# Moving an inverse to VectorE's transposes, a norm to a block's delay, and a last norm to fused steps

## The chip, the core and the metric

One NeuronCore of one Trainium2 chip runs the whole program. The time is device microseconds from start to end of an execution, the median of some runs. The engines work side by side, each through its own queue in order: TensorE (PE, with PEld for its weight loads), VectorE (DVE), ScalarE (ACT), GpSimd (POOL), and SyncE (SP), which issues most DMAs. [...]

## What is computed

One layer of a backbone on 640 tokens, 128 of a prompt and 512 of a sample, 1024 features, fp32:

```python
h = x * (1 + sc1) + sh1
proj = h @ p['w_in']
q, k, v, rw, gates = jnp.split(proj, ...)
o_att = diff_attention(q, k, v, lam)          # 4 heads, then rms_norm
# bidirectional RWKV7, 8 heads of 64, for each direction and token:
sa = jnp.einsum('bhvk,bhk->bhv', S, a_t)
S = S * w_t[:, :, None, :] + sa[..., None] * b_t[:, :, None, :] + v_t[..., None] * k_t[:, :, None, :]
y_t = jnp.einsum('bhvk,bhk->bhv', S, r_t)
...
mix = (ga * (o_att @ p['w_o_attn']) + gb * o_rw) @ p['w_out']
x = layer_norm(ALPHA * x + g1 * mix, p['ln1_g'], p['ln1_b'])
h = x * (1 + sc2) + sh2
u, val = jnp.split(h @ p['w_up'], 2, axis=-1)
u = prev * cw[0] + u * cw[1] + nxt * cw[2] + p['conv_b']
f = (jax.nn.gelu(u) * val) @ p['w_down']
x = layer_norm(ALPHA * x + g2 * f, p['ln2_g'], p['ln2_b'])
```

Outputs are x of both token groups, the prompt's keys and values, and the final states S of both directions.

## The kernel before

Tokens stand in five blocks of 128 (block 0 is the prompt). Matrix operands are split into a high and a low part, so that a product is three: high by high, high by low, low by high.

**The mixing stage** (about 60 to 710 us) interleaves two kinds of work on PE by hand. One is the input projection: a generator `flow` that yields after each product (L215, 128x320), and `pull(n)` takes n of them. These products are the fillers here. The other is the scan, in four pairs of heads, i = 0 to 3. The scan is chunked: 64 tokens a chunk, 10 chunks a direction, so 40 chunk matrices a pair (two heads, two directions). Each needs the inverse of a triangular 64x64 matrix. In the loop over pairs:

- `rw_b` (through `side()`) prepares decays and keys; `rw_c` multiplies them into the 40 chunk matrices (L642) and masks them on VectorE (L648) into the tile MS, 128 partitions x 40 chunks x 128.
- `rw_i` inverts the two 32x32 diagonal blocks of each chunk matrix. 64 products with the identity (L706) turn the blocks so that chunks lie on partitions (X, 104 partitions: chunks of one block on 0 to 39, of the other on 64 to 103); 4 copies evict them (L710). 60 VectorE operations (L716, L718) eliminate. 8 PE transposes (L729) and 16 copies (L733, half on ACT) bring the blocks back into MS. Between the 30 elimination steps stand a `side()` and a `pull(4)`.
- `rw_m` joins the blocks (transpose L741, products L747 and L755), forms the chunk operators and walks the states (L839, L841), ten steps with `pull(14)` each. It ends with the final states' transposes (L864), a copy fo and two DMAs to new_s.
- `rw_e` forms the outputs y (L888), `rw_d` the transposed operands, `rw_f` the norm of the scan's output (L899 to L923), which it writes to yr_dram.

`side()` advances the first of the listed side generators until it is done. After the loop `rw_e(3)`, `pull(12)`, and `rw_f(3)` with `pull(8)` a step run, then what is left of the fillers. Then the stage's pools are closed, and attention loads queries and keys (L1097) and starts with L1086 and L1116.

**The first norm.** `w_out`'s second half of columns is multiplied for the five blocks (L1249), each into a PSUM bank of its own. For each block follow the residual (L1277, L1278), the statistics, the norm itself (L1326, on VectorE), 8 transposes (L1332) and the operands oph and opl of the up-products (L1335 to L1343, L224). A scheduler fixes the order on each engine when the program is built, from the order of the code and its own estimates. The first up-products are L1413.

**The last norm.** The down weights come in groups of 5, 5, 5 and 7 blocks of 128. For the last group's second half of columns 2 of 7 blocks go over all five token blocks first, the other 5 (TJS) keep their weights in tiles (wdh, wdl) and run token block by token block (L1447 to L1449), and `finish` then does each block's norm: L1461, L1462, statistics, nm, and per half L1476 (ACT, once L1474 on VectorE), L1477 (VectorE), L1478 (VectorE for the five halves listed in BD, else GpSimd), and a DMA out.

Of the kernel before, what the change touches and what calls it, by code (L numbers as in the profile page):

```python
# [47 lines left out]
TJS = 5  # L48
# [18 lines left out]
def tile_layer(ctx, tc, x_prompt, x_sample, cache_k, cache_v, state_rwkv, c, c_ctx, w_ada, b_ada, w_in,  # L67
# [625 lines left out]
    def rw_i(i):  # L693
        MS = R[i]["MS"]

        X = rp.tile([104, 32, 32], F32, name="X", tag="st")
        tmp = rp.tile([104, 256], F32, name="tmpx", tag="tmpx")
        nc.gpsimd.memset(X[32:64], 0.0)
        prev = None
# [24 lines left out]

        for y in (1, 0):
            ps = bank(psR, "m", 2)
            for u in (3, 2, 1, 0):
                c0 = 128 * (4 * y + u)
                prev = chain(prev, pq(nc.tensor.transpose(out=ps[:, 104 * u:104 * u + 104], in_=Xf[:, c0:c0 + 128], identity=ident[0:104, 0:104])))  # L729
            for q in range(4):  # L730
                for b in range(2):
                    t0 = 32 * b + 16 * y + q
                    (nc.scalar.copy if b else nc.vector.tensor_copy)(  # L733
                        out=MS[32 * b:32 * b + 32, :, t0:t0 + 13:4],
                        in_=ps[32 * q:32 * q + 32, 0:416].rearrange("p (u r) -> p r u", u=4)[:, 64 * b:64 * b + 40, :])
        pull(16)

    def rw_m(i):
# [104 lines left out]
        for v in range(10):  # L843
# [16 lines left out]
            pull(14)  # L860
        ps = bank(psR, "m", 2)
        fo = rp.tile([64, 2, P], F32, name="fo", tag="tmpx")
        for d in range(2):
            pq(nc.tensor.transpose(out=ps[0:64, d * P:(d + 1) * P], in_=FS[:, d, :], identity=ident))  # L864
        nc.scalar.copy(out=fo, in_=ps[0:64, 0:256].rearrange("p (d k) -> p d k", d=2))
        for d in range(2):
            nc.sync.dma_start(out=new_s[d, 2 * i:2 * i + 2].rearrange("e v k -> v e k"), in_=fo[:, d, :].rearrange("p (e k) -> p e k", e=2))

        R[i].update(UV=UV, ST=ST)

    def rw_e(i):
# [18 lines left out]
        R[i].update(y=y, gup=gup)  # L890

# [704 lines left out]
```

## Time and profile before

| | |
|---|---|
| median of 3 runs | 1432.46 us (1431.22 to 1436.12) |
| the profiled execution | 1437.26 us, its span 1435.2 us, mean granted clock of PE 0.932 |
| PE busy | 1287.7 us, 90% of the span |
| VectorE busy | 911.8 us, 64% |
| ScalarE, GpSimd busy | 563.7 and 564.9 us, 39% each |
| chain that ended last | PE 38%, VectorE 16%, issue 5%, GpSimd 4%, ScalarE 3%, DMA 2% |

Times in rows are microseconds from the start of the span. The span is about 2 us shorter than the execution's own time. A PE row's duration covers the whole pipeline, so that rows follow each other faster than they last: the step from one start to the next is what a product costs. Idle time in brackets stands ahead of an instruction, with the instruction that ended it. [...]

### The profile page before, as it was taken

Reading aid. Unit: us, or ns where it says so; the run is one execution under the profiler, and the core shown is the slowest. Engines: PE = TensorE matmul, PEld = TensorE weight load, DVE = VectorE, ACT = ScalarE, POOL = GpSimd, SP = SyncE. Lnnn points to the kernel's source line nnn. Section 1 sums busy time; section 2 is a strip of 40 time slices with the busy share of each in tenths; the row PEclk is TensorE's granted clock in tenths of the full one; section 3 lists DMA queues with packets and bytes.
Section 4 is the critical chain, followed back from the end, with each engine's and each line's share of the span. In section 5 each row is a group of like instructions: output and inputs, shape, how many; then the busy total and the mean of one; then the engine's idle time right before and its main releaser. Section 6 shows DMA issues by size and latency. Waiting matters only on the chain.

```text
span 1435.2 us, 27691 instructions
## 1 busy us (share of the span) xinstructions
PE 1287.7 (90%) x11105; PEld 1140.6 (79%) x11105; DVE 911.8 (64%) x1683; ACT 563.7 (39%) x1158; POOL 564.9 (39%) x424
## 2 busy tenths in 40 slices
PE   6998898988888999999979889968999999999994
PEld 5887887877777888889867777758988989989983
DVE  2365847584847563831266523597897987778777
ACT  3442533344324441533355412354543433434432
POOL 3252217331643232212220235546654735536623
PEclk9997998898988998999989999978999999999997
DMA  9411212220222111212656787513232232322222
GB/s 306 125 49 34 63 30 69 78 76 28 64 72 70 51 33 51 77 50 75 195 160 204 265 265 265 171 60 102 74 104 73 74 96 66 90 66 79 69 67 88
DMA packets 157459, 144.64 MB, mean 101 GB/s; under 512 B 10490, under 2 KB 128020, under 8 KB 157332
## 3 DMA queue, kind: packets, MB, share of 16 engines
q1 hardware_dynamic: 147490, 127.85, 29.0%
q10 hardware_dynamic: 9842, 15.03, 3.1%
q8 instruction: 87, 1.43, 0.4%
q14 instruction: 40, 0.33, 0.1%
HBM read 121.06 MB, written 19.69 MB: 98 GB/s over the span
## 4 chain that ended last, share of the span: by engine, by line
PE 38%; DVE 16%; issue 5%; POOL 4%; ACT 3%; DMA 2%; SPq 0%; ACTq 0%; DVEq 0%; POOLq 0%
PE ps_d L1413 8%; PE ps_d L215 6%; PE ps_x L215 4%; PE ps_e L1413 3%; PE acc L1449 2%; PE acc L1447 2%; PE acc L1448 2%; DVE sums L1386 2%; DVE zacc L1462 1%; PE acc L1249 1%; PE T L1140 1%; POOL wl L224 1%; DMA ws<-in_w_out_dram 1%; DVE X L718 1%; DVE tmpx L716 1%
## 5 line engine op out<-in xcount | busy, mean ns | idle before, releaser
L187 POOL TENSOR_TENSOR wl<-ws,wh 128x512 fp32r<-128x512 f32 x100 | 138.5, 1386 | 400.5 <-ACT wh L186 349.4
L224 POOL TENSOR_TENSOR wl<-sums,wh 128x512 fp32r<-128x512 f32 x88 | 137.4, 1568 | 38.3 <-ACT wh L223 36.5
L1413 PE MATMUL ps_d<-oph,wh 128*128 128x320 f32 x440 | 138.5, 315 | 10.6 <-DVE u L1425 5.0
L224 POOL TENSOR_TENSOR wl<-wu,wh 128x512 fp32r<-128x512 f32 x63 | 88.9, 1412 | 142.9 <-ACT wh L223 129.6
L1413 PE MATMUL ps_d<-oph,wl 128*128 128x320 f32 x440 | 137.5, 313 | 0.6 <-POOL wl L224 0.6
L1413 PE MATMUL ps_d<-opl,wh 128*128 128x320 f32 x440 | 137.3, 312 | 0.7 <-DVE opl L224 0.7
L186 ACT CAST wh<-ws 128x512 fp32r<-128x512 f32 x100 | 61.4, 618 | 171.3 <-PE ps_d L215 66.9
L215 PE MATMUL ps_x<-hl,wh 128*128 128x320 f32 (+1 forms) x304 | 104.5, 344 | 0.0
L215 PE MATMUL ps_x<-hh,wh 128*128 128x320 f32 (+1 forms) x304 | 104.5, 344 | 0.0
L215 PE MATMUL ps_x<-hh,wl 128*128 128x320 f32 (+1 forms) x304 | 104.2, 343 | 0.0
L215 PE MATMUL ps_d<-hl,wh 128*128 128x320 f32 (+1 forms) x304 | 103.7, 341 | 0.0
L215 PE MATMUL ps_d<-hh,wl 128*128 128x320 f32 (+1 forms) x304 | 103.6, 341 | 0.0
L215 PE MATMUL ps_d<-hh,wh 128*128 128x320 f32 (+1 forms) x304 | 103.4, 340 | 0.0
L1413 PEld LDWEIGHTS ps_d<-oph,wh 128*128 128x128 f32 x440 | 83.7, 190 | 15.1 <-ACT wh L223 7.7
L1413 PEld LDWEIGHTS ps_d<-opl,wh 128*128 128x128 f32 x440 | 83.7, 190 | 2.0 <-POOL hf L1343 1.1
L1413 PEld LDWEIGHTS ps_d<-oph,wl 128*128 128x128 f32 x440 | 83.7, 190 | 1.4 <-POOL wl L224 1.2
L223 ACT CAST wh<-sums 128x512 fp32r<-128x512 f32 x88 | 54.6, 620 | 65.2 <-PE ps_e L1413 25.4
L1447 PE MATMUL acc<-wh,gh 128*128 128x512 f32 x195 | 77.5, 398 | 2.6 <-ACT gh L223 2.6
L1448 PE MATMUL acc<-wl,gh 128*128 128x512 f32 x195 | 77.3, 397 | 0.0
L1449 PE MATMUL acc<-wh,gl 128*128 128x512 f32 x195 | 76.1, 397 | 0.5 <-DVE gl L224 0.5
L223 ACT CAST wh<-wu 128x512 fp32r<-128x512 f32 x63 | 39.1, 621 | 73.2 <-PE acc L1449 30.1
L215 PEld LDWEIGHTS ps_x<-hh,wh 128*128 128x128 f32 x304 | 63.4, 209 | 2.6 <-issue 1.1
(439 smaller groups left out, 3641.2 us busy)
## 6 DMA issues: line engine op xcount, KB each, us to landing
wu<-in_w_up_dram SPq DMA_DIRECT2D x42, 512.0 KB
ws<-in_w_in_dram SPq DMA_DIRECT2D x76, 256.0 KB
wa<-in_w_ada_dram SPq DMA_DIRECT2D x24, 512.0 KB
ws<-in_w_down_dram SPq DMA_DIRECT2D x44, 256.0 KB
wa<-in_w_ada_dram SPq DMA_DIRECT2D x8, 1024.0 KB
ks<-qk_dram SPq DMA_DIRECT2D x32, 192.0 KB
g_dram<-tg ACTq DMA_DIRECT2D x16, 320.0 KB
tg<-g_dram SPq DMA_DIRECT2D x16, 320.0 KB
```

Of the source, the lines that this page charges most:

```text
L186: nc.scalar.copy(out=wh, in_=ws)
L187: (lo_eng or nc.gpsimd).tensor_tensor(out=wl, in0=ws, in1=wh.bitcast(F32), op=ALU.subtract)
L215: pq(nc.tensor.matmul(pd, w[:, k, :], x[:, g, sl], start=g == 0 and z == 0, stop=g == kb - 1 and z == 2))
L223: nc.scalar.copy(out=hi, in_=src)
L224: (lo_eng or nc.vector).tensor_tensor(out=lo, in0=src, in1=hi.bitcast(F32), op=ALU.subtract)
L716: nc.vector.tensor_tensor(out=tv, in0=X[:, j:j + 1, 0:j].broadcast_to([104, n, j]), in1=X[:, j + 1:32, j:j + 1].broadcast_to([104, n, j]), ...
L718: nc.vector.tensor_tensor(out=X[:, j + 1:32, 0:j], in0=X[:, j + 1:32, 0:j], in1=tv, op=ALU.add)
L1386: (nc.vector if q in USM else nc.gpsimd).tensor_tensor(out=o, in0=x0, in1=x1, op=op)
L1413: nc.tensor.matmul(ps, w[:, k, :], x[:, b, k, :], start=k == 0 and z == 0, stop=k == 3 and z == 2)
L1447: nc.tensor.matmul(acc, a_h, wh, start=first, stop=False)
L1448: nc.tensor.matmul(acc, a_h, wl, start=False, stop=False)
L1449: nc.tensor.matmul(acc, a_l, wh, start=False, stop=last)
```

## The change

1. `rw_i`: the 64 products, the 4 copies, the 8 PE transposes and the 16 copies are gone. Four stream transposes on VectorE turn the blocks into X, four turn them back. Each takes 32 partitions x 32 chunks x 32; a chunk lies 512 bytes from the next in MS, while X is contiguous. X has 128 partitions now, four groups: chunks 0 to 31 and 8 to 39 of each diagonal block, so that 24 chunks are inverted twice. The elimination's free sizes stay. A `pull(8)` stands behind each of the four first transposes (before, four times 6), and `pull(26)` at the end (16).
2. `side()` takes the side generators in turn.
3. `rw_m` pulls 16 instead of 14 fillers a step. Its last part, transposes of the final states, copy and DMAs, stands at the end of `rw_e`.
4. `pull(40)` ahead of the first `rw_c`.
5. First norm: one chain fixes PE's order. The products of block t, then the transposes of block t - 1. The norm is done by ScalarE with a small VectorE step for its bias. 12 products that nobody reads stand ahead of the last block's transposes and 10 behind them, reading the mix operand and the first output weights.
6. Last norm: per half two fused VectorE steps, (z - mean) * g and (. * rstd) + b. nm, the ScalarE steps and GpSimd's additions are gone. TJS is 7: all blocks of the group run token block by token block.

```diff
-TJS = 5
+TJS = 7
@@ side
-            if next(sides[0], None) is None:
-                del sides[0]
+            f = sides.pop(0)
+            if next(f, None) is not None:
+                sides.append(f)
@@ rw_i
-        X = rp.tile([104, 32, 32], F32, name="X", tag="st")
...
-        for y in range(2):
-            ps = bank(psR, "m", 2).rearrange("p (t s) -> p t s", s=32)
-            for t in range(16):
-                for b in range(2):
-                    rows = slice(32 * b, 32 * b + 32)
-                    prev = chain(prev, pq(nc.tensor.matmul(ps[64 * b:64 * b + 40, t, :], MS[rows, :, 32 * b + 16 * y + t], ident[rows, rows], start=True, stop=True)))
-                if t % 8 == 7:
-                    pull(6)
-            for b in range(2):
-                (nc.scalar.copy if b else nc.vector.tensor_copy)(out=X[64 * b:64 * b + 40, 16 * y:16 * y + 16, :], in_=ps[64 * b:64 * b + 40])
+        X = rp.tile([P, 32, 32], F32, name="X", tag="st")
+        tmp = rp.tile([P, 256], F32, name="tmpx", tag="tmpx")
+        turns = [(X[32 * g:32 * g + 32], MS[32 * (g // 2):32 * (g // 2) + 32, 8 * (g % 2):8 * (g % 2) + 32, 32 * (g // 2):32 * (g // 2) + 32].rearrange("p c t -> p t c")) for g in range(4)]
+        for x, m in turns:
+            nc.vector.transpose(out=x, in_=m)
+            pull(8)
...
-        for y in (1, 0):
...
-        pull(16)
+        for x, m in turns:
+            nc.vector.transpose(out=m, in_=x)
+        pull(26)
@@ rw_m
-            pull(14)
...
+            pull(16)
@@ the loop over pairs
+        else:
+            pull(40)
@@ first norm
+        def normed(t5):
+            for k in range(KB):
+                after[0] = mix_products(accs[t5], t5, wo[k], k, after[0])
...
-            nc.vector.tensor_scalar(out=z1, in0=z1, scalar1=mv[:, 0:1], scalar2=mv[:, 1:2], op0=ALU.subtract, op1=ALU.mult)
+            nm = po2.tile([P, 1], F32, name="nm1", tag="nm1", bufs=2)
+            nc.vector.scalar_tensor_tensor(out=nm, in0=mv[:, 0:1], scalar=-1.0, in1=mv[:, 1:2], op0=ALU.mult, op1=ALU.mult)
+            nc.scalar.activation(out=z1, in_=z1, func=AF.Identity, scale=mv[:, 1:2], bias=nm)
...
+        for t5 in range(5):
+            normed(t5)
+            if t5:
+                operand(t5 - 1)
...
+        def warm(n):
+            for _ in range(n):
+                after[0] = chain(after[0], nc.tensor.matmul(idle, mh[:, 0, 0:P], wo[0][0], start=True, stop=True))
+        warm(12)
+        operand(4)
+        warm(10)
@@ finish
+                nc.vector.scalar_tensor_tensor(out=z[:, zs], in0=z[:, zs], scalar=mv[:, 0:1], in1=lnb2[:, 0, zs], op0=ALU.subtract, op1=ALU.mult)
+                nc.vector.scalar_tensor_tensor(out=z[:, zs], in0=z[:, zs], scalar=mv[:, 1:2], in1=lnb2[:, 1, zs], op0=ALU.mult, op1=ALU.add)
```

The order on the engines changes most in three places. VectorE at the start of the first pair's inverse (MS the masked chunk matrices, ps_m and ps_ch PSUM banks of PE, vs the attention values), before:

```order
L648 TENSOR_TENSOR MS<-ps_ch,mk 128x512
L710 COPY X<-ps_m 40x512
L246 TENSOR_SCALAR bs<-ps_d 128x2
L710 COPY X<-ps_m 40x512
L712 MEMSET X 104x32
L716 TENSOR_TENSOR tmpx<-X 104x30
L718 TENSOR_TENSOR X<-X,tmpx 104x30
```

and in the changed kernel:

```order
L649 TENSOR_TENSOR MS<-ps_ch,mk 128x512
L701 STREAM_TRANSPOSE X<-MS 32x1024
L937 COPY vs<-ps_d 128x512
L937 COPY vs<-ps_d 128x128
L701 STREAM_TRANSPOSE X<-MS 32x1024 x3
L246 TENSOR_SCALAR bs<-ps_x 128x2
L703 MEMSET X 128x32
L707 TENSOR_TENSOR tmpx<-X 128x30
L709 TENSOR_TENSOR X<-X,tmpx 128x30
```

The copies that waited for PE gave way to transposes that read MS directly.

PE in the last pair's norm, `rw_f(3)` (bl, sd, rx, ta, sg, gup are that norm's; ps_x and ps_d with hh, hl, wh, wl the fillers'), before around its first product:

```order
L215 MATMUL ps_x<-hh,wh 128x322
L215 MATMUL ps_x<-hl,wh 128x322
L215 MATMUL ps_x<-hh,wl 128x322
L513 MATMUL ps_m<-bl,sd 128x2 x5
L215 MATMUL ps_x<-hh,wh 128x320
L215 MATMUL ps_x<-hl,wh 128x320
L215 MATMUL ps_x<-hh,wl 128x320
```

and in the changed kernel, to attention's first products:

```order
L215 MATMUL ps_d<-hh,wh 128x320
L215 MATMUL ps_d<-hl,wh 128x320
L215 MATMUL ps_d<-hh,wl 128x320
L514 MATMUL ps_m<-bl,sd 128x2 x5
L530 MATMUL ps_m<-ident,rx 128x128 x2
L530 MATMUL ps_m<-ident,rx 128x64 x2
L530 MATMUL ps_m<-ident,rx 128x128 x2
L896 MATMUL ps_m<-ta,bl 128x320 x2
L903 MATMUL ps_m<-sg,gup 128x320 x2
L1069 MATMUL T<-l_7437,ones_7440 128x1
L1099 MATMUL S<-ks,qs 128x64 x5
```

Of the 224 fillers that stood behind `rw_e(3)` 32 are left, and none stands behind the norm's L514.

VectorE at the very end (bmv the statistics, lnb the last norm's factors, zacc the five blocks), before:

```order
L1470 SCALAR_TENSOR_TENSOR nm<-bmv 128x1
L1236 BN_AGGR bmv<-st_14766 128x2
L1237 TENSOR_SCALAR bmv<-bmv 128x1
L1470 SCALAR_TENSOR_TENSOR nm<-bmv 128x1
L1474 TENSOR_SCALAR zacc<-zacc,bmv 128x512
L1477 TENSOR_TENSOR zacc<-zacc,lnb_14755 128x512 x4
L1478 TENSOR_TENSOR zacc<-zacc,lnb_14755 128x512 x3
```

and in the changed kernel:

```order
L1219 BN_AGGR bmv<-st_14443 128x2
L1220 TENSOR_SCALAR bmv<-bmv 128x1
L1479 SCALAR_TENSOR_TENSOR zacc<-zacc,bmv,lnb_14432 128x512 x2
L1480 SCALAR_TENSOR_TENSOR zacc<-zacc,bmv,lnb_14432 128x512 x2
L1220 TENSOR_SCALAR bmv<-bmv 128x1
L1479 SCALAR_TENSOR_TENSOR zacc<-zacc,bmv,lnb_14432 128x512 x2
L1480 SCALAR_TENSOR_TENSOR zacc<-zacc,bmv,lnb_14432 128x512 x2
```

Each block now has four fused steps on VectorE, and no other engine takes part but for GpSimd's power of the statistics.

## Rows read from the trace of the kernel before

**Rows 1.** Busy time of the engines by stretch: stretch, its length, engines, clock, DMA.

```profile
core 0: us, PE busy (x) PEld busy (x) DVE busy (x) ACT busy (x) POOL busy (x), PEclk, DMA share, GB/s
72.00:670.00 598.00, 534.21 (x6370) 475.53 (x6369) 361.81 (x767) 229.17 (x487) 202.23 (x149) 0.90 0.19 57
100.00:120.00 20.00, 13.92 (x99) 12.38 (x100) 13.58 (x21) 4.45 (x9) 9.34 (x6) 0.76 0.18 54
```

**Rows 2.** PE's waits, 72 to 709 us: total, times, longest, in us.

```profile
PE ps_m L747 <- DVE Y L741: 8.8, 4, 4.1
PE ps_m L642 <- DVE MS L648: 6.1, 1, 6.1
PE ps_ch L839 <- DVE ST L841: 4.6, 4, 2.2
```

**Rows 3.** The inverse: groups, durations by line (min/median/max), L729 alone, VectorE's timeline (start, us).

```profile
L706 PE MATMUL ps_m<-ident,MS 32*40 32x32 f32 x512 | 21.2, 240 | 1.8 <-DVE MS L648 1.8
L733 DVE COPY MS<-ps_m 32x160 f32<-32x160 f32 x32 | 13.3, 434 | 10.8 <-PE ps_m L729 5.3 <-ACT MS L733 4.8
...
L741 DVE STREAM_TRANSPOSE Y<-MS x4: 1490/1500/1500, 173.2 to 612.0; 32x1280 f32<-32x1280 f32 x4
...
310.00:330.00 20.00, 0.88 (x8) 0.82 (x8) 0.91 0.24 73
...
124.47 0.68 DVE L648 TENSOR_TENSOR MS<-ps_ch,mk 128x512 f32<-128x512 f32 x1
137.36 0.22 DVE L718 TENSOR_TENSOR X<-X,tmpx 104x58 f32<-104x58 f32 x1
165.72 0.22 DVE L718 TENSOR_TENSOR X<-X,tmpx 104x58 f32<-104x58 f32 x1
173.21 1.50 DVE L741 STREAM_TRANSPOSE Y<-MS 32x1280 f32<-32x1280 f32 x1
```

**Rows 4.** PE's timeline among fillers: start, us, instruction.

```profile
660.08 0.31 PE L215 MATMUL ps_x<-hh,wh 128*128 128x320 f32 x1
660.23 0.31 PE L215 MATMUL ps_x<-hl,wh 128*128 128x320 f32 x1
```

**Rows 5.** Timelines of PE, VectorE and SyncE at the end of the mixing stage.

```profile
671.55 0.70 PE L899 MATMUL ps_m<-y,bl 128*128 128x320 f32 x2
692.80 0.55 DVE L923 SCALAR_TENSOR_TENSOR yc<-yc,vT,ps_m 128x320 f32<-128x320 f32 x1 [0.31 <-PE ps_m L922]
696.90 1.65 SPq L1097 DMA_DIRECT2D qs<-qk_dram  x2
702.65 2.50 SPq L1097 DMA_DIRECT2D ks<-qk_dram  x4
708.66 0.38 PE L1086 MATMUL T<-l,ones 1*128 1x1 f32 x2
```

**Rows 6.** First norm: durations of L1326; timelines of all engines; stretch 972 to 978.

```profile
L1326 DVE TENSOR_SCALAR zacc<-zacc,bmv x5: 812/1216/1736, 927.3 to 959.0; 128x1024 f32<-128x1024 f32 x5
954.64 0.99 SPq L1259 DMA_DIRECT2D wu<-in_w_up_dram  x2
959.02 1.74 DVE L1326 TENSOR_SCALAR zacc<-zacc,bmv 128x1024 f32<-128x1024 f32 x1 [0.66 <-POOL bmv L1238]
960.42 1.06 ACT L1367 ACTIVATE lnb<-lnb 128x1024 f32<-128x1024 f32 x1 [1.32 <-DMA lnb<-in_ln_g_dram]
960.90 1.94 PE L1332 MATMUL ps_d<-ident,zacc 128*128 128x128 f32 x8 [6.29 <-DVE zacc L1326]
966.80 0.60 PE L1413 MATMUL ps_d<-opl,wh 128*128 128x320 f32 x1 [0.74 <-DVE opl L224]
972.00:978.00 6.00, 5.36 (x20) 5.20 (x20) 3.17 (x4) 0.92 (x2) 4.95 (x4) 0.50 0.94 254
```

**Rows 7.** Last norm: VectorE's timeline; durations of L1435, the fused form elsewhere.

```profile
1404.83 0.69 DVE L1461 TENSOR_TENSOR fz<-acc,gb 128x512 f32<-128x512 f32 x1 [1.17 <-PE acc L1449]
1430.10 1.88 DVE L1478 TENSOR_TENSOR zacc<-zacc,lnb 128x512 f32<-128x512 f32 x3
...
L1435 DVE SCALAR_TENSOR_TENSOR ctmp<-ur,vT,ctmp x22: 873/1178/1928, 986.5 to 1382.9; 128x642 f32<-128x642 f32 x22
```

More of the change, by code (lines that the diff above doesn't have):

```diff
@@ L723, in rw_i @@
             pull(4)
-        for y in (1, 0):
[L726 to L735, printed above, removed]
-        pull(16)
+        for x, m in turns:
+            nc.vector.transpose(out=m, in_=x)
+        pull(26)
     def rw_m(i):
@@ L859, in rw_m @@
             side(3)
-            pull(14)
[L861 to L869, printed above, removed]
+            pull(16)
+        R[i].update(UV=UV, ST=ST, FS=FS)
     def rw_e(i):
@@ L890, in rw_e @@
         R[i].update(y=y, gup=gup)
+        FS = R[i]["FS"]
+        ps = bank(psR, "m", 2)
+        fo = rp.tile([64, 2, P], F32, name="fo", tag="tmpx")
+        for d in range(2):
+            pq(nc.tensor.transpose(out=ps[0:64, d * P:(d + 1) * P], in_=FS[:, d, :], identity=ident))
+        nc.scalar.copy(out=fo, in_=ps[0:64, 0:256].rearrange("p (d k) -> p d k", d=2))
+        for d in range(2):
+            nc.sync.dma_start(out=new_s[d, 2 * i:2 * i + 2].rearrange("e v k -> v e k"), in_=fo[:, d, :].rearrange("p (e k) -> p e k", e=2))
     def rw_f(i):
@@ L1244, in five_banks, with mix_products @@
         return [psF.tile([P, 512], F32, name=f"acc{t}", tag=f"acc{t}") for t in range(5)]
-    def mix_products(ps, t5, wo, k):
+    def mix_products(ps, t5, wo, k, prev=None):
         a_h, a_l = mh[:, k, t5 * P:(t5 + 1) * P], ml[:, k, t5 * P:(t5 + 1) * P]
         for q, (lhs, w) in enumerate(((a_h, wo[0]), (a_h, wo[1]), (a_l, wo[0]))):
-            nc.tensor.matmul(ps, lhs, w, start=k == 0 and q == 0, stop=k == KB - 1 and q == 2)
+            prev = chain(prev, nc.tensor.matmul(ps, lhs, w, start=k == 0 and q == 0, stop=k == KB - 1 and q == 2))
+        return prev
     wup = ctx.enter_context(tc.tile_pool(name="wup", bufs=1, reuse_waits="tile"))
@@ L1318, in tile_layer @@
         accs = five_banks()
-        for t5 in range(5):
-            v = 0 if t5 == 0 else 1
+        after = [None]
+        def normed(t5):
             for k in range(KB):
-                mix_products(accs[t5], t5, wo[k], k)
+                after[0] = mix_products(accs[t5], t5, wo[k], k, after[0])
             residual(accs[t5], t5, zs, gb_b)
@@ L1325, in tile_layer, with operand @@
             mv = norm_stats(z1, po2)
-            nc.vector.tensor_scalar(out=z1, in0=z1, scalar1=mv[:, 0:1], scalar2=mv[:, 1:2], op0=ALU.subtract, op1=ALU.mult)
+            nm = po2.tile([P, 1], F32, name="nm1", tag="nm1", bufs=2)
+            nc.vector.scalar_tensor_tensor(out=nm, in0=mv[:, 0:1], scalar=-1.0, in1=mv[:, 1:2], op0=ALU.mult, op1=ALU.mult)
+            nc.scalar.activation(out=z1, in_=z1, func=AF.Identity, scale=mv[:, 1:2], bias=nm)
+        def operand(t5):
+            v = 0 if t5 == 0 else 1
+            z1 = zacc[:, t5, :]
             hf = po2.tile([P, KB, P], F32, name="hf2", tag="hf2", bufs=2)
@@ L1331, in tile_layer @@
                 for k in range(4):
-                    nc.tensor.transpose(out=pt[:, k * P:(k + 1) * P], in_=z1[:, (k0 + k) * P:(k0 + k + 1) * P], identity=ident)
+                    after[0] = chain(after[0], nc.tensor.transpose(out=pt[:, k * P:(k + 1) * P], in_=z1[:, (k0 + k) * P:(k0 + k + 1) * P], identity=ident))
                 for k in range(4):
@@ L1347, in tile_layer @@
                 split(oph[:, q:q + n, :, cols], opl[:, q:q + n, :, cols], src, nc.gpsimd if i in (LOP if t5 < 4 else LOZ) else None)
+        for t5 in range(5):
+            normed(t5)
+            if t5:
+                operand(t5 - 1)
+        idle = psF.tile([P, 512], F32, name="idle", tag="extra")
+        def warm(n):
[4 more added lines that the diff above has]
+        warm(10)
         load_up(0, None)
@@ L1540, in tile_layer @@
                 for e, (g, wh, wl) in enumerate(ends):
-                    down_one(accs[t5], t5, g, wh, wl, False, e == TJ - 1)
+                    down_one(accs[t5], t5, g, wh, wl, n == TJ and e == 0, e == TJ - 1)
                 finish(t5, accs[t5], sts[t5])
```

18 lines of the change are left out of this document (3 added, 15 removed).

## The prediction

> **What bounds the kernel now.** I read the busy shares by stretch, then the waits of TensorE (PE), then the inverse, the end of the mixing stage and the two norms. Over the mixing stage (72 to 670 us) PE is busy 534.2 of 598 us, VectorE 361.8, ScalarE 229.2 [rows 1]. PE is the bound, but 63.8 us of it are waits, and they lie in lumps: 6.1 us between 100 and 120 us alone. [rows 2] names the releasers: once, for 6.1 us, the mask product L648; four times, 8.8 us in all, the transpose L741 that closes an inverse. The reader should see that in these places VectorE's serial chain sets the pace, because the fillers (L215) standing there have run out. At the first norm PE stands 6.29 us ahead of the last transposes, and then works at half the clock [rows 6]. At the end VectorE works alone [rows 7].
>
> **The change part by part.** A filler step costs 660.23 - 660.08 = 0.15 us at the full clock, 0.147 over a longer run of such rows [rows 4]; every moved filler is counted with it.
>
> *Inverse, PE side.* Per pair of heads 64 small products (128 records) and 8 transposes go: 21.2 us for four pairs, and 0.88 us a pair at the full clock, 3.5 for four [rows 3]. That is 24.7 us of PE work, 6.2 a pair. 18 fillers a pair come in, 18 x 0.147 = 2.65 us; they are the same work, done earlier.
>
> *Inverse, VectorE side.* In the first pair the chain runs from the end of the last mask product, 124.47 + 0.68 = 125.15, to the end of L741, 173.21 + 1.50 = 174.7: 49.6 us. The elimination is 29.7 of them (its second addition starts at 137.36, its second last at 165.72, and each end adds under a microsecond) [rows 3]; 1.5 are L741, and the other 18.4 are products, evictions, transposes, 16 copies. Eight stream transposes of 32x1024 take their place. The nearest row is L741 itself, 32x1280 in 1.50 us, 1.17 ns an element: 1.2 us each, 9.6 a pair. But L741 reads runs of 32 elements, while the new ones step 512 bytes from element to element on one side. Bound above: the strided evictions L733 take 434 ns for 160 elements, 2.7 ns an element [rows 3], so 2.8 us each; no reason makes a wider step cheaper than 1.2. With L733's fixed share taken off, its elements cost perhaps 1.9 ns (an estimate), 2.0 us each. I take 1.2: the elimination step at 137.36 works on 58 elements that lie in pairs 128 bytes apart, the one at 165.72 on two runs of 29, and both take 0.22 us [rows 3]. No step shows in VectorE's time there.
>
> [...]
>
> With 1.2 us the chain is 4.8 + 29.7 + 4.8 + 1.5 = 40.8 us, 8.8 shorter. PE has 6.2 - 2.65 = 3.6 us less to do in the same stretch. So a pair gains 3.6 if PE sets it and 8.8 if the chain does; I take 6, and 24 us for the four, 14 and 35 as ends. VectorE itself gives up some 4.8 us of copies a pair and takes 9.6; with 361.8 of 598 us busy it has the room.
>
> *Later in a pair.* `rw_m` gets 20 more fillers, 2.9 us a pair, 11.8 in all. What they can fill are waits like L839's for L841, 4.6 us [rows 2]: I count 4, so a loss of 8 (4 to 12). The final-state transposes, their copy and two output DMAs move to the end of `rw_e`; nothing on SyncE's queue waits for them there: 0. Taking the side steps in turn reorders the same instructions: 0, with 2 us either way.
>
> *40 fillers ahead of the first masks.* 40 x 0.147 = 5.9 us go into the wait of 6.1 [rows 2]. They fit; the gain is booked in the tail.
>
> *The end of the mixing stage.* All in all 192 fillers have left it, 28.2 us: 224 stood behind `rw_e(3)`, 32 remain. Before, the last pair's L899 starts at 671.55, its last step on VectorE ends at 692.80 + 0.55 = 693.35, and attention's first product starts at 708.66 [rows 5]: 37.1 us with PE always at work. Now the fillers end early in that stretch, and the rest is bare latency. The last pair's norm keeps all its hops, but none queues behind up to a dozen fillers; I estimate 15 us for the 21.8 (ends 12 and 21.8). The query and key loads cannot start before the stage's pool is closed: they are issued from 696.90 on, 3.5 us behind 693.35, twelve until 702.65 + 2.50 = 705.15 [rows 5]. The first product needs the first six; with some 2 to 3 us of flight I put it 10 us (8 to 13) behind the norm, where 15.3 passed. 37.1 becomes about 25: 12 us gained (4 to 16). The other 16 of the 28 are lost as idle time of PE.
>
> Sum of the stage: 24 - 8 + 0 + 12 = 28 us (10 to 38). Cross-check: 24.7 us of PE work are gone, so 28 asks for 3 us less idle time in all, with some 14 new at the end and so 17 less of the 63.8.
>
> *First norm.* The 128x1024 step leaves VectorE. Its five took 0.81 to 1.74 us, 1.22 in the middle [rows 6]; the four ahead of the last block sum to some 4.1, five small steps of about 0.1 come back: 3.6 us earlier. The last took 1.74 us from 959.02; on ScalarE the price is L1367's 1.06, same shape [rows 6], with the small step and a handover about 1.5. So block 4's transposes start about 4 us earlier, and steady up-products at 962.8, not 966.80: 4 us (2 to 7). PE's strict order costs nothing: already now PE waits 6.29 us for that block [rows 6], so VectorE sets it. [...] 22 unread products fill much of the idle time ahead; I take 3 (0 to 5). They read the mix operand, so the loads into its place, issued at 954.64 [rows 6], leave about 6 us later; block 0 does not use them, and they have some 10 us to spare: 0, and 3 us if that cover is gone. Sum 7 us (2 to 12).
>
> *Last norm.* VectorE's chain runs from 1404.83 to 1430.10 + 1.88 = 1431.98 [rows 7]. After: a product, an addition, statistics and four fused steps of 128x512 a block, and two small ones. Three such steps, undisturbed, take 1.88 us, 0.63 each; the fused form takes 0.873 at best for 642 elements, 0.69 in proportion, overlap included [rows 7]. With 0.63 a block is 7 x 0.63 + 0.25 = 4.65, five 23.3. By the new order the first bank is complete two products sooner (place 56 of 105, not 58), 0.4 us. End 1404.4 + 23.3 = 1427.7: 4 us gained (0 with 0.8 us a fused step, 6 with 0.55). The powers on GpSimd hide behind the first fused pair. The seven weight pairs are all needed by place 55, as now by 57.
>
> **Total** 28 + 7 + 4 = 39 us. The profiled execution has 1437.3 us, 1398 after; it lies 4.8 above the median of the runs, 1432.5, and taken off that the forecast is 1393.
>
> **Rivals.**
> *The strided transposes cost about 2.0 us.* A pair's chain is then 47.2 us and gains 1 to 2 instead of 6: some 19 less, 1412. For it L733's 2.7 ns an element; against it the equal 0.22 us.
> *The tail stays exposed.* The last pair's norm keeps its 21.8 us, the loads take 13: 2 instead of 12; `rw_m`'s fillers cover nothing (4 less), and the clock does not come back at the first norm (3 less): 1410. For it: the loads leave only at 696.90. Against it: the norm's hops on PE now wait behind fillers.
> *VectorE becomes the bound of the inverse, and it is slower.* At 2.8 us a transpose a pair's chain is 53.6 us, 4 more than now and 12.8 more than forecast: 51 us for four pairs, of which PE's own pace hides some 5: 39 - 46, 1439. It decides from about 2.6 us each. Against it: every other VectorE row is cheaper by the element.
> *The change does not do what it says*: the fillers move into stretches without idle time, the fused steps are no faster, the unread products only hold PE. Inverse 14, `rw_m` -12, end of the stage 4, norms 2: 1424.
>
> **How the numbers follow.** Forecast 0.60 (1380 to 1405), strided price 0.13, exposed tail 0.13, no effect 0.07, VectorE the bound 0.07. The range 1376 to 1424 holds the first three and half of the fourth. Within 0.3%, 4.3 us (about what a measurement of this kernel can tell from no change), lie parts of the last two: 0.05; slower 0.08; faster 0.87.
>
> **What would show it.** Stream transposes of 1.2 us; under 1 us of PE idle between 100 and 120 us; two gaps of PE of about 10 us each, inside the last pair's norm and ahead of attention; steady up-products at a clock near 1.00; the last VectorE step 23 us behind the first of the last norm. It is wrong if the transposes take 2 us, or if PE stands for over 25 us around the start of attention.

## The result and the profile after

Before took 1434.29 us in the comparison (4 runs, 1431.22 to 1441.08), the changed kernel 1412.93 (4 runs, 1409.86 to 1416.34). The ratio is 0.9845 with the interval 0.98 to 0.989: some 21 us are gained where 39 were forecast. The time lies in the range and 20 us above the forecast.

The profiled execution took 1411.21 us, its span 1409.1 us, mean granted clock 0.944 of PE's full speed. The page's busy times:

```profile
PE 1253.5 (89%) x10583; PEld 1109.9 (79%) x10583; DVE 945.7 (67%) x1674; ACT 542.9 (39%) x1114; POOL 556.9 (40%) x415
```

PE has 34 us less to do (1287.7 before), VectorE 34 us more (911.8 before). The stretches, in the columns of [rows 1] and with its first stretch again:

```profile
72.00:670.00 598.00, 529.63 (x6043) 477.01 (x6042) 401.63 (x766) 220.65 (x469) 210.37 (x155) 0.92 0.21 62
100.00:120.00 20.00, 18.82 (x152) 17.33 (x152) 14.99 (x25) 6.69 (x14) 11.44 (x8) 0.95 0.29 85
125.00:175.00 50.00, 36.81 (x323) 35.21 (x324) 47.38 (x85) 21.72 (x43) 11.06 (x8) 0.88 0.18 51
```

The third row is the first pair's inverse. The same stretch of before, not read for the prediction:

```profile
125.00:175.00 50.00, 44.81 (x442) 42.09 (x446) 35.57 (x85) 24.67 (x51) 10.19 (x8) 0.86 0.18 52
```

The reader should compare the third figures. VectorE went from 35.6 to 47.4 busy us out of 50: it is now the bound there, while PE dropped to 36.8. The new and the kept transposes of VectorE, in the changed kernel (durations min/median/max in ns, then first and last start):

```profile
L701 DVE STREAM_TRANSPOSE X<-MS x16: 1879/1994/2053, 123.1 to 565.6; 32x1024 f32<-32x1024 f32 x16
...
L716 DVE STREAM_TRANSPOSE MS<-X x16: 1875/1979/2047, 163.3 to 604.6; 32x1024 f32<-32x1024 f32 x16
...
L722 DVE STREAM_TRANSPOSE Y<-MS x4: 1499/1500/1501, 173.0 to 606.8; 32x1280 f32<-32x1280 f32 x4
```

A turn costs 1.99 or 1.98 us, 1.94 ns an element, where the closing transpose L722 pays 1.17. PE's waits from 72 to 709 us, as in [rows 2], and the row of the first of them:

```profile
PE ps_m L728 <- DVE Y L722: 20.5, 4, 9.6
PE S L1099 <- DMA ks<-qk_dram: 7.7, 4, 4.0
...
PE ps_ch L820 <- DVE ST L822: 6.5, 3, 2.9
```

```profile
174.58 1.29 PE L728 MATMUL ps_m<-Y,MS 32*32 32x32 f32 x80 [9.63 <-DVE Y L722]
```

The wait for the closing transpose grew from 8.8 to 20.5 us. The mask wait of 6.1 us is gone from the longest, and PE is busy 18.8 of 20 us between 100 and 120.

Where the span's 26.1 us went, by landmarks in the two traces. A pair's inverse is counted from the end of its last mask product to the end of its closing transpose; the rest of a pair runs to the next pair's last mask product, the last pair's to the end of `rw_e(3)`.

| stretch | before | after | difference | forecast |
|---|---|---|---|---|
| up to the first pair's last mask | 125.2 | 123.2 | -2.0 | in the tail |
| four inverses | 49.6 + 62.9 + 58.0 + 51.9 = 222.4 | 51.4 + 51.2 + 53.1 + 49.0 = 204.7 | -17.7 | -24 |
| four rests | 322.2 | 338.1 | +15.9 | +8 |
| end of `rw_e(3)` to attention's steady products | 42.7 | 32.4 | -10.3 | -12 |
| from there to the first steady up-product | 254.3 | 248.0 | -6.4 | -4 |
| to the last norm's first step | 438.0 | 436.5 | -1.5 | -3 (clock) |
| last norm on VectorE | 27.2 | 23.2 | -4.0 | -4 |

Medians show 21.4 of these 26.1 us: the profiled execution of before lies above its median, as the prediction took into account, and that of after 1.7 below.

### The profile page after: what moved, and what is told of

Same layout as the page of the kernel before. It is cut to its first block, busy times and chain, and to the rows that moved or that the text cites. A ratio compares the mean times of both kernels' runs of the same rounds, so it can differ in the third digit from the quotient of the medians.

```text
span 1409.1 us, 26546 instructions
## 1 busy us (share of the span) xinstructions
PE 1253.5 (89%) x10583; PEld 1109.9 (79%) x10583; DVE 945.7 (67%) x1674; ACT 542.9 (39%) x1114; POOL 556.9 (40%) x415
## 5 line engine op out<-in xcount | busy, mean ns | idle before, releaser
L224 POOL TENSOR_TENSOR wl<-sums,wh 128x512 fp32r<-128x512 f32 x88 | 137.4, 1569 | 37.4 <-ACT wh L223 34.0
L224 POOL TENSOR_TENSOR wl<-wu,wh 128x512 fp32r<-128x512 f32 x63 | 89.8, 1426 | 141.8 <-ACT wh L223 130.7
L215 PE MATMUL ps_x<-hh,wh 128*128 128x320 f32 (+1 forms) x304 | 101.4, 334 | 0.0
L1455 PE MATMUL acc<-wh,gh 128*128 128x512 f32 x185 | 73.6, 398 | 2.7 <-ACT gh L223 2.7
L1456 PE MATMUL acc<-wl,gh 128*128 128x512 f32 x185 | 73.5, 397 | 0.1
L1457 PE MATMUL acc<-wh,gl 128*128 128x512 f32 x185 | 72.3, 397 | 0.5 <-DVE gl L224 0.5
L215 PEld LDWEIGHTS ps_d<-hh,wh 128*128 128x128 f32 x304 | 62.6, 206 | 2.6 <-issue 0.9
```

The costliest lines, as they stand in the source:

```text
L215: pq(nc.tensor.matmul(pd, w[:, k, :], x[:, g, sl], start=g == 0 and z == 0, stop=g == kb - 1 and z == 2))
L224: (lo_eng or nc.vector).tensor_tensor(out=lo, in0=src, in1=hi.bitcast(F32), op=ALU.subtract)
L1455: nc.tensor.matmul(acc, a_h, wh, start=first, stop=False)
L1456: nc.tensor.matmul(acc, a_h, wl, start=False, stop=False)
L1457: nc.tensor.matmul(acc, a_l, wh, start=False, stop=last)
```

## The experiments

The theory from the profile: the turns cost 2.0 us because they go over single elements that lie far apart, and this is what keeps the inverse long. Rivals: a 32x1024 turn costs 2.0 us in any order; VectorE's time is hidden anyway, and the loss is that of the moved fillers; the first norm's part failed.

**The step taken away.** The turns read and write runs of 32 neighbours, so that other numbers are inverted.

```diff
-..., 32 * (g // 2):32 * (g // 2) + 32].rearrange("p c t -> p t c")) for g in range(4)]
+..., 32 * (g // 2):32 * (g // 2) + 32]) for g in range(4)]
```

> Edit: the eight turning transposes of a pair read and write runs of 32 neighbouring elements, like the transpose that closes the inverse, in place of steps of 512 bytes; what is inverted is then not the right block, so the outputs of the scan are not the reference's. Everything else is the changed kernel, 1412.9 us. Theory P (the price of the step, 1.98 us a transpose in the changed kernel, is what the forecast lacked): 1.2 us each, PE's wait for the closing transpose falls from 20.5 to under 10 us, total 1393 to 1400 us. Theory Q (the transposes hide beside PE, the loss sits in the extra fillers and in the idle end of the stage): transposes cheaper, but total 1408 to 1413.

Measured 1385.66 us, ratio 0.9655 (0.9625 to 0.9686). VectorE's groups in it (busy us, mean ns, idle time ahead), and PE's wait for the closing transpose:

```profile
L716 DVE STREAM_TRANSPOSE MS<-X 32x1024 f32<-32x1024 f32 x16 | 19.8, 1235 | 0.5
L701 DVE STREAM_TRANSPOSE X<-MS 32x1024 f32<-32x1024 f32 x16 | 19.7, 1233 | 0.2
```

```profile
PE ps_m L728 <- DVE Y L722: 13.4, 3, 9.2
```

1.23 us a turn: the prediction's 1.2 is the price of neighbours. The changed kernel's two groups sum to 31.7 + 31.4 = 63.1 us; 23.6 us go from VectorE, and the time falls by 27 us: VectorE's time was not hidden. `rw_e(3)` ends at 637.7, not 666.0, so all of the gain arises in the mixing stage. Theory P has the right kind and too small a size: the time lies 7 us below its range, and PE's wait for the closing transpose fell to 13.4 us, not under 10. Why the time falls by some 4 us more than VectorE gives up is not shown.

**Pairs of elements.** As the last, but in runs of two elements, the next run 512 bytes on.

```diff
-..., 32 * (g // 2):32 * (g // 2) + 32].rearrange("p c t -> p t c")) for g in range(4)]
+..., 32 * (g // 2):32 * (g // 2) + 32].rearrange("p c (t w) -> p t c w", w=2)) for g in range(4)]
...
-            nc.vector.transpose(out=x, in_=m)
+            nc.vector.transpose(out=x.rearrange("p (t u) (c w) -> p t u c w", u=2, w=2), in_=m.rearrange("p t (u c) w -> p t u c w", u=2))
...
-            nc.vector.transpose(out=m, in_=x)
+            nc.vector.transpose(out=m.rearrange("p t (u c) w -> p t u c w", u=2), in_=x.rearrange("p (t u) (c w) -> p t u c w", u=2, w=2))
```

> Edit to the changed kernel: the turning transposes step by 512 bytes only after two neighbouring elements (runs of 8 bytes); the blocks that are turned are then not the right ones, so the outputs of the scan are not the reference's. Theory (the price falls on single elements, as the elimination's first step with 30 single elements takes 0.21 us against 0.19 for 30 neighbours, while pairs cost nothing): 1.23 us a transpose, total 1383 to 1390 as with plain turns. Rival (the price is one of each 512-byte jump): 1.5 to 1.7 us a transpose, total 1395 to 1404.

Measured 1386.39 us, 0.9674 (0.9654 to 0.9695), not to be told from runs of 32, and in the range of the theory. The two turns:

```profile
L701 DVE STREAM_TRANSPOSE X<-MS x16: 1222/1236/1237, 122.2 to 543.3; 32x1024 f32<-32x1024 f32 x16
...
L716 DVE STREAM_TRANSPOSE MS<-X x16: 1233/1234/1240, 160.4 to 578.4; 32x1024 f32<-32x1024 f32 x16
```

So the 512-byte jump by itself is not paid for (1236 ns in runs of two, 1233 in runs of 32), only an element that stands alone behind such a jump (1994 ns in the changed kernel).

**The step given to ScalarE.** Seven of the eight turns work in place on X, which is contiguous, and a copy on ScalarE takes the step; the closing transpose stands in `rw_i`, behind the turns.

```diff
-            nc.vector.transpose(out=x, in_=m)
+            if g:
+                nc.scalar.copy(out=x, in_=m)
+            nc.vector.transpose(out=x, in_=x if g else m)
...
-            nc.vector.transpose(out=m, in_=x)
+            last = chain(last, nc.vector.transpose(out=x, in_=x))
+            nc.scalar.copy(out=m, in_=x)
+        last = chain(last, nc.vector.transpose(out=Y11, in_=MS[0:32, :, 0:32]))
...
```

> Edit to the changed kernel: seven of a pair's eight turning transposes work in place on the contiguous tile X (runs of 32 elements); the steps of 512 bytes are taken by seven ScalarE copies of 32x1024 (three ahead of the elimination, four behind it), and the closing transpose follows the fourth. Everything is computed. P (price of the step on VectorE sets the inverse): 1.23 us a transpose instead of 1.98, some 5 us less on the chain of a pair, one copy's latency of 1 to 2 us added at either end; total 1388 to 1398 against 1412.9, and 1385.7 with plain turns. Rival: a ScalarE copy with steps costs as much as the transpose did (2 us and more) and the chain only changes its engine; total 1405 to 1415.

Measured 1405.64 us, 0.9815 (0.9777 to 0.9854): in the range of the rival, above that of P. Its copies and turns:

```profile
L702 ACT COPY X<-MS x12: 1989/2040/2162, 122.6 to 558.9; 32x1024 f32<-32x1024 f32 x12
...
L721 ACT COPY MS<-X x16: 1897/1970/2057, 162.2 to 600.5; 32x1024 f32<-32x1024 f32 x16
...
L720 DVE STREAM_TRANSPOSE X<-X x16: 1232/1234/1242, 160.9 to 598.5; 32x1024 f32<-32x1024 f32 x16
```

The turns in place cost 1.23 us, and ScalarE now pays 2.0 us for the same step, where its activation over 1024 neighbours takes 1.06 [rows 6]: the price belongs to the access, not to the transpose. Four copies in a row on ScalarE are a chain too: in the first pair they run from 162.2 to 171.0 us, nearly as long as the four turns of the changed kernel (163.3 to 173.0). That so little comes of it for this reason is read from the trace, not tried.

**The closing transpose earlier.** L722 reads the upper diagonal blocks alone, which the first two back-turns complete; it is put behind them.

```diff
-        for x, m in turns:
-            nc.vector.transpose(out=m, in_=x)
+        for g, (x, m) in enumerate(turns):
+            last = chain(last, nc.vector.transpose(out=m, in_=x))
+            if g == 1:
+                last = chain(last, nc.vector.transpose(out=Y11, in_=MS[0:32, :, 0:32]))
...
-        nc.vector.transpose(out=Y11, in_=MS[0:32, :, 0:32])
```

> Edit: of the four transposes back into the chunk matrices the two that the joining step needs come first, then the closing transpose, then the other two. VectorE's work is the same, the first joining product can start 3.9 us earlier in each pair. P (PE waits behind the serial chain of VectorE): the wait of 20.5 us falls to 5 to 9, total 1399 to 1407. Q: total within 3 us of 1412.9.

Measured 1408.72 us, 0.9813 (0.9781 to 0.9846): about 4 us better than the change in the medians, with overlapping intervals, and just outside both ranges that were named. PE's wait for this transpose fell from 20.5 us to 9.7, where P had 5 to 9.

```profile
PE ps_m L732 <- DVE Y L720: 9.7, 3, 7.5
```

**`rw_m` with 14 fillers a step again.**

```diff
-            pull(16)
+            pull(14)
```

> Edit: 14 instead of 16 fillers in each of the ten state steps of a pair, as before; 80 fillers (11.8 us) stay for the end of the mixing stage. P: the steps had nothing to hide the extra fillers behind, while at the end PE stands for some 20 us in the last pair's norm and for loads; total 1403 to 1409, with the stretch from the closing transpose to the end of the outputs 2 to 3 us shorter in each pair. Q (the extra fillers were free): total 1412 to 1420, the end longer by what the steps lose.

Measured 1418.33 us, 0.9881 (0.9833 to 0.9929): in the range of Q, not in that of P, though the interval overlaps that of the change. In the traces `rw_e(3)` ends at 664.7 instead of 666.0: 80 fillers, 11.8 us of PE work, cost only 1.3 us there. Attention's first product with keys and queries (L1099) comes at 696.2, not 690.1. So the extra fillers did fill idle time, and taken away they stand at the end.

**The inverse alone.** The kernel before with the new `rw_i` and nothing else of the change.

```diff
@@ rw_i
-        X = rp.tile([104, 32, 32], F32, name="X", tag="st")
...
+        for x, m in turns:
+            nc.vector.transpose(out=x, in_=m)
+            pull(8)
...
+        for x, m in turns:
+            nc.vector.transpose(out=m, in_=x)
+        pull(26)
```

> Edit: the kernel before with the new inverse alone (transposes on VectorE, pulls of 8 and 26). PE has 24.7 us less work, VectorE some 45 us more. P: the four inverse stretches together 8 to 18 us shorter, a part of it lost to PE's half clock behind the waits; total 1420 to 1430 against 1434.3 for the kernel before. Q (the inverse itself gives what was forecast and the other edits lose it): 1408 to 1416.

Measured 1423.22 us, 0.9905 (0.9869 to 0.9941): 12 us less than before in the medians, the larger part of what the change gains.

**The side steps in the order of before, and each norm as before**, four kernels:

```diff
@@ side steps
-            f = sides.pop(0)
-            if next(f, None) is not None:
-                sides.append(f)
+            if next(sides[0], None) is None:
+                del sides[0]
@@ first norm as before
-            nc.scalar.activation(out=z1, in_=z1, func=AF.Identity, scale=mv[:, 1:2], bias=nm)
+            nc.vector.tensor_scalar(out=z1, in0=z1, scalar1=mv[:, 0:1], scalar2=mv[:, 1:2], op0=ALU.subtract, op1=ALU.mult)
...
@@ no unread products
-        warm(12)
...
-        warm(10)
@@ last norm as before
-TJS = 7
+TJS = 5
...
-                nc.vector.scalar_tensor_tensor(out=z[:, zs], in0=z[:, zs], scalar=mv[:, 0:1], in1=lnb2[:, 0, zs], op0=ALU.subtract, op1=ALU.mult)
+                nc.vector.tensor_tensor(out=z[:, zs], in0=z[:, zs], in1=lnb2[:, 0, zs], op=ALU.mult)
...
```

> Edit: the changed kernel with the side steps of before (the first listed generator until it is done). The forecast put nothing on it, 2 us either way: 1411 to 1415. Rival: taking them in turn is what delays the first pair after its inverse (87.5 us from the closing transpose to the end of the outputs, 78.9 before) and what shortens the second pair's inverse (51.2, 62.9 before): the first falls by 5 to 9 us, the second grows by 6 to 12, total 1412 to 1420.

> Edit: the changed kernel with the first norm of the kernel before (norm on VectorE, no fixed order on PE, no unread products). By the forecast's term it would be 7 us slower (1418 to 1422). By the two traces, 44.1 us against 42.8 from the first block's last product to the steady up-products and 1 to 3 us back by the clock, the term is small: 1411 to 1416.

> Edit: the changed kernel without its 22 unread products at the first norm. If they keep PE's clock up, as forecast: PE's lower clock lasts 2 to 3 us longer there, steady up-products begin no earlier, total 1 to 3 us more than 1412.9. Rival (they stand in front of the up-products and PE's clock falls all the same, as the granted 0.50 in 935 to 941 and 947 to 953 us suggests): up-products begin up to 1.5 us earlier, total 1410 to 1413.

> Edit: the changed kernel with the last norm of the kernel before (ScalarE and GpSimd share it, TJS 5). The forecast's term: 4 us, total 1415 to 1419; in the traces VectorE's chain runs 23.2 us after the change and 27.1 before. Rival (fused steps of 0.66 us each cost what the shared ones did): 1411 to 1414.

| | us | ratio to before | interval |
|---|---|---|---|
| the change | 1412.93 | 0.9845 | 0.98 to 0.989 |
| side steps as before | 1414.59 | 0.9867 | 0.9838 to 0.9896 |
| first norm as before | 1412.22 | 0.9849 | 0.9824 to 0.9875 |
| no unread products | 1413.22 | 0.9858 | 0.9833 to 0.9883 |
| last norm as before | 1418.51 | 0.9891 | 0.9873 to 0.9909 |

The first three experiments can't be told from the change: the first norm's whole rebuilding is worth nothing measurable. In the traces the steady up-products begin at 946.35 us in the changed kernel, and no later with the first norm of before or without the unread products:

```profile
946.11 0.61 PE L1397 MATMUL ps_d<-opl,wh 128*128 128x320 f32 x1 [0.74 <-DVE opl L224]
...
946.31 0.61 PE L1419 MATMUL ps_d<-opl,wh 128*128 128x320 f32 x1 [0.92 <-DVE opl L224]
```

The rival on the side steps does not show either: with their old order the first pair's outputs end 87.3 us behind its closing transpose, 87.5 with the new one, and the second inverse takes 49.1 and 51.2 us. Without the new last norm the median is 5.6 us higher. The intervals overlap, but the traces say the same: VectorE's chain there takes 26 us against 23.2.

**Three remedies together.** The earlier closing transpose, two of the first turns in place behind copies on ScalarE, 17 fillers a step.

```diff
-            nc.vector.transpose(out=x, in_=m)
+            if g > 1:
+                nc.scalar.copy(out=x, in_=m)
+            nc.vector.transpose(out=x, in_=x if g > 1 else m)
...
-            pull(16)
+            pull(17)
```

> Edit: the joining order of join_early (1408.7 us), two of the four first transposes in place on X behind ScalarE copies that run beside the other two, and 17 fillers a state step, which brings the last 32 fillers forward from the end of the stage. Expected from the two steps: chain of a pair 1.5 us shorter, 4 to 5 us of fillers into waits of the state steps: 1398 to 1406. Rival (fillers run out in the last pair, and PE stands there and ahead of attention instead): 1406 to 1412.

Measured 1405.12 us, 0.9801 (0.9774 to 0.9828): in the range that was expected, but not to be told from the earlier closing transpose alone.

**Chunks woven in pairs.** Two chunks lie element by element side by side in MS, so that every turn finds runs of two. Masks write and PE reads MS with a step of 8 bytes.

```diff
-        MS = rp.tile([P, 4 * NCH, P], F32, name="MS", tag="ms")
+        MS = rp.tile([P, 2 * NCH, P, 2], F32, name="MS", tag="ms")
...
-        turns = [(X[...], MS[..., 8 * (g % 2):8 * (g % 2) + 32, ...].rearrange("p c t -> p t c")) for g in range(4)]
+        turns = [(X[...], MS[..., 4 * (g % 2):4 * (g % 2) + 16, ..., :].rearrange("p c t w -> p t c w")) for g in range(4)]
...
-            nc.vector.transpose(out=x, in_=m)
+            nc.vector.transpose(out=x.rearrange("p t (c w) -> p t c w", w=2), in_=m)
...
-   MS[0:32, ix, 32:64]
+   MS[0:32, ix // 2, 32:64, ix % 2]
```

with the earlier closing transpose, and every other use of MS indexed in the same way.

> Edit: join_early with another layout of the chunk matrices: two chunks are woven together element by element, so that every access of a turning transpose takes two neighbours (8 bytes) before it steps; everything is computed. All other users read or write with a step of 8 bytes: the mask products, the closing transpose, and PE for some 900 small products a kernel. If two elements in a row are free on PE as well as on VectorE: 1.23 us a transpose, total 1378 to 1388 (1386 for pairs on the wrong blocks, less up to 4 from the joining order). Rival (PE reads an operand with a step of 8 bytes at half its speed or less): the transposes are cheaper, PE's small products on MS longer, total 1395 to 1430.

Measured 1384.04 us (5 runs, 1382.27 to 1386.4), 0.9651 (0.9632 to 0.967): 51 us below before, 29 below the change. Its turns, its masks, the output products, into which MS flows as the moving operand (first L865, then 64 of them in a row), and the loads of MS as weights (L777); in the second fence masks, output products and weight loads of the changed kernel:

```profile
L701 DVE STREAM_TRANSPOSE X<-MS x16: 1222/1236/1239, 122.4 to 538.6; 32x1024 f32<-32x1024 f32 x16
...
L649 DVE TENSOR_TENSOR MS<-ps_m,mk x16: 672/692/696, 114.4 to 533.4; 128x512 f32<-128x512 f32 x16
...
L865 PE MATMUL ps_m<-MS,UV x320: 218/220/274, 248.5 to 632.5; 128*64 128x64 f32 x160
...
630.64 2.09 PE L865 MATMUL ps_m<-MS,UV 128*64 128x64 f32 x64
...
L777 PEld LDWEIGHTS ps_ch<-AT,MS x320: 132/135/221, 177.5 to 609.9; 64*64 64x64 f32 x160
```

```profile
L649 DVE TENSOR_TENSOR MS<-ps_m,mk x16: 676/691/693, 115.0 to 558.1; 128x512 f32<-128x512 f32 x16
...
L861 PE MATMUL ps_m<-MS,UV x320: 222/222/270, 256.9 to 663.8; 128*64 128x64 f32 x160
...
661.90 2.08 PE L861 MATMUL ps_m<-MS,UV 128*64 128x64 f32 x64
...
L773 PEld LDWEIGHTS ps_ch<-AT,MS x320: 129/135/228, 186.3 to 641.2; 64*64 64x64 f32 x160
```

Turns at 1.24 us, and these rows show no price of the new layout: masks 692 against 691 ns, 64 products 2.09 against 2.08 us, weight loads 135 ns in both.

## Why the prediction came out as it did

**The failed step is the price of a turn.** The prediction had the right price among its own: 1.2 us by L741, 2.8 by the strided evictions L733, and 2.0, its estimate from L733 without the fixed share. It gave that share no size; L246's rows of two elements from PSUM took 127 to 161 ns before, which would leave L733's elements 1.7 to 1.9 ns, the turns 1.7 to 2.0 us. It chose 1.2, because two elimination steps on 58 elements took 0.22 us each. The runs show 1.98 and 1.99; transposes of 2 us it had itself named as a sign of being wrong. The two steps could not show the effect: the elements of the first lie in pairs, and pairs cost nothing, as the second experiment shows (1236 against 1233 ns a turn). The trace of before held a pair of rows that could. The first elimination step works on 30 elements that stand alone, 128 bytes apart, the last on 30 neighbours:

```profile
136.86 0.21 DVE L718 TENSOR_TENSOR X<-X,tmpx 104x30 f32<-104x30 f32 x1
...
166.20 0.19 DVE L718 TENSOR_TENSOR X<-X,tmpx 104x30 f32<-104x30 f32 x1
```

20 ns over 30 elements are 0.7 ns each, and 1.17 + 0.7 is some 1.9 ns, what the turns then cost. The changed kernel has the same two rows:

```profile
132.31 0.21 DVE L709 TENSOR_TENSOR X<-X,tmpx 128x30 f32<-128x30 f32 x1
...
163.12 0.19 DVE L709 TENSOR_TENSOR X<-X,tmpx 128x30 f32<-128x30 f32 x1
```

The rows are rounded to 10 ns; to the nanosecond they are 211 and 191 before, 210 and 191 after. By itself one pair of short rows is weak; it agrees with the measured turns: 1.94 ns for an element that stands alone, 1.21 for one of two neighbours.

**The rival came true.** "The strided transposes cost about 2.0 us" had 1412, and 1412.93 was measured. Its mechanism is shown by the first two experiments. The time lies in the stated range because the range was drawn to hold this rival, which had a chance of 0.13. That the number fits so well is partly chance: it counted 19 us for the dearer turns, and the experiment shows 27; other terms make up for it. At the chosen price the kernel takes 1385.7, 7 below the forecast, so the gains of the other steps together were put too low.

**VectorE "has the room": wrong.** The prediction read 361.8 of 598 us, a mean over the stage [rows 1]. In the inverse VectorE had 35.6 of 50 us already, and takes 47.4 now. A pair's inverse was a VectorE chain before and is one still; so it gains or loses nearly all that the turns cost, not the 6 us between two bounds. With runs of two the four inverses take 180.0 us, 42 less than before, above the end of 35 that the prediction gave. It had measured one pair, 49.6 us, for all four; the second and third took 62.9 and 58.0. In that first pair the chain takes 46.6 us with turns of 1.23 us, not the 40.8 of its sum: VectorE's steps for other work (L937, L422 to L424) stand between the turns and in the elimination.

**Fillers in `rw_m`: right in kind, wrong in size.** They were to cost 8 us net and cost 1.3 by the experiment that takes them away. The rests of the pairs are 16 us longer all the same; with the new inverse alone they grow by 1.4 only (to 323.6 us). With 14 fillers they take 327.3 and the inverses 7 us more than in the change: what a filler takes in one stretch it gives back in the next. The two stretches of the account must be read as a sum, -1.8 us after the change and -28.2 with runs of 32 in the turns (180.0 and 336.4), where the forecast had -16.

**The 40 fillers ahead of the first masks** did what was said: 18.8 busy us between 100 and 120, 1.2 idle, where under 1 was named. In the trace 2 us were gained there.

**The end of the stage: right.** 12 us were forecast, 10.3 measured. PE's, VectorE's and SyncE's rows:

```profile
667.95 0.70 PE L880 MATMUL ps_m<-y,bl 128*128 128x320 f32 x2
...
676.18 2.93 PE L530 MATMUL ps_m<-ident,rx 128*128 128x128 f32 x12 [3.04 <-ACT rx L525]
...
682.80 1.00 DVE L904 SCALAR_TENSOR_TENSOR yc<-yc,vT,ps_m 128x320 f32<-128x320 f32 x2
...
684.26 1.15 SPq L1080 DMA_DIRECT2D qs<-qk_dram  x2
...
689.77 2.51 SPq L1080 DMA_DIRECT2D ks<-qk_dram  x4
...
690.13 0.39 PE L1099 MATMUL S<-ks,qs 128*128 128x64 f32 x1 [3.96 <-DMA ks<-qk_dram]
```

The stretch from 680 to 700 us, in the columns of [rows 1]:

```profile
680.00:700.00 20.00, 8.65 (x27) 6.42 (x26) 6.10 (x18) 2.01 (x7) 0.00 (x0) 0.59 0.74 189
```

The norm, from its first product at 667.95 to its last step on VectorE at 683.8, takes 15.9 us, forecast 15. The first load leaves half a microsecond later, and PE waits for it 3.96 us: L1099 comes 22.2 us behind the norm's first product, forecast about 25, but more waits for loads follow. From 680 to 700 us PE works 8.65 of 20 us, at a clock of 0.59. That is the bare latency which the prediction described, though the gap inside the norm is 3.04 us, not about 10.

**The first norm: no gain.** 7 us were forecast, and two experiments show none. The rows of the last block and of the up-products:

```profile
929.68 3.03 PE L1351 MATMUL idle<-woh,mh 128*128 128x512 f32 x12
...
929.50 0.69 DVE L1261 SCALAR_TENSOR_TENSOR gm<-acc,gb 128x512 f32<-128x512 f32 x1
...
933.36 0.68 DVE L1262 SCALAR_TENSOR_TENSOR zacc<-zacc,gm 128x512 f32<-128x512 f32 x1
...
936.64 1.24 ACT L1314 ACTIVATE zacc<-zacc,nm,bmv 128x1024 f32<-128x1024 f32 x1 [0.38 <-DVE nm L1313]
...
937.93 1.97 PE L1325 MATMUL ps_d<-ident,zacc 128*128 128x128 f32 x8 [5.22 <-ACT zacc L1314]
...
940.72 0.95 DVE L224 TENSOR_TENSOR opl<-hf,oph 128x256 fp32r<-128x256 f32 x1
...
945.52 2.10 DVE L224 TENSOR_TENSOR opl<-hf,oph 128x512 fp32r<-128x512 f32 x2
...
946.35 0.60 PE L1421 MATMUL ps_d<-opl,wh 128*128 128x320 f32 x1 [1.01 <-DVE opl L224]
```

The stretch 947 to 953 us, as that of before in [rows 6], then the same without the unread products:

```profile
947.00:953.00 6.00, 4.19 (x14) 3.39 (x14) 4.77 (x7) 2.41 (x5) 4.80 (x6) 0.50 0.93 306
...
947.00:953.00 6.00, 4.46 (x16) 3.68 (x16) 4.77 (x7) 1.98 (x4) 4.81 (x6) 0.50 0.54 191
```

After the 12 unread products PE still stands 5.22 us, 6.29 before [rows 6], and the clock in the first up-products is 0.50 as it was, with the unread products or without. The 3 us that the forecast put on these products no run shows: without them the median is 1413.22 us, with them 1412.93. Block 4's transposes were to start 4 us earlier. Counted from block 0's first residual step (L1277 at 924.02 before, L1261 at 902.59 now) they come 35.3 us later, 36.9 before: 1.5 us are gained. One thing that holds them up is block 4's residual: its second step L1262 starts 3.2 us after the end of the first, L1261, and in between VectorE makes block 2's operands. From the last transposes to the steady up-products it takes 937.93 to 946.35 = 8.4 us, where it was 960.90 to 966.80 = 5.9 [rows 6]. In between VectorE works off block 3's operands, which the new order puts a block later (L224 at 940.72 and before), and then block 4's. Both delays are read from the rows, not tried by themselves. The prediction priced what left VectorE and not what the delay put in its way.

**The last norm: right.** 4 us forecast, 4.0 in the traces, 5.6 in the medians. Start and end of VectorE's chain, and a fused step:

```profile
1382.89 1.39 DVE L1469 TENSOR_TENSOR fz<-acc,gb 128x512 f32<-128x512 f32 x2 [1.53 <-PE acc L1457]
...
1403.33 1.41 DVE L1479 SCALAR_TENSOR_TENSOR zacc<-zacc,bmv,lnb 128x512 f32<-128x512 f32 x2
1404.65 1.41 DVE L1480 SCALAR_TENSOR_TENSOR zacc<-zacc,bmv,lnb 128x512 f32<-128x512 f32 x2
```

```profile
L1479 DVE SCALAR_TENSOR_TENSOR zacc<-zacc,bmv,lnb x10: 740/744/748, 1387.3 to 1404.0; 128x512 f32<-128x512 f32 x10
```

23.2 us, forecast 23.3. Two steps take 1404.65 - 1403.33 = 1.32 us from start to start, 0.66 each, a little more than the 0.63 taken.

**Still open.** From attention's steady products to the first steady up-product the traces gain 6.4 us, though the end of the first norm became no shorter. PE's granted clock is higher there after (0.96 against 0.91 from 710 to 800 us), but the two stretches don't hold the same work. No run isolates this, and up to 4.8 us may belong to the one execution of before that was profiled, which lies that far above the median the prediction started from.

## To carry to other kernels

Single fp32 elements 512 bytes apart cost VectorE's transposes here 1.6 times the time of neighbours (1.98 against 1.23 us), and ScalarE 2.0 us where an activation over 1024 neighbours took 1.06; before a move is planned around such a step, look for a layout that gives runs of two. When a price has to be taken from a nearby row, ask whether that row has the property in question: 58 elements in pairs say nothing about 1024 that stand alone. Whether an engine has room is read in the stretch to which work is added, not in a mean over the stage.

## What the runs showed of the hardware

- A 32x1024 fp32 stream transpose takes 1.23 us where both sides have runs of two or more, 1.98 us where one side steps from single element to single element at 512 bytes, reading or writing. A ScalarE copy of that shape with the same step takes 1.97 to 2.04 us.
- Runs of two elements (8 bytes), 512 bytes apart, cost no more than runs of 32: 1236 against 1233 ns.
- A step of 8 bytes between single elements costs nothing that shows: VectorE's masked evictions, which write with it, 692 against 691 ns, 64 PE products that stream MS with it 2.09 against 2.08 us, PE's weight loads from MS 135 ns in both.
- 22 unread products around a wait of PE changed neither the clock behind it, 0.50 with and without them, nor the time by anything that shows (ratio 0.9858 without them, 0.9845 with them).
